# Modulation chunks 4 to 17 as multiply-adds on VectorE in place of matmuls on TensorE

## The chip, the cores and the metric

One core of a Trainium2 chip runs the whole kernel. The metric is the device time of one launch in microseconds (us). The engines are TensorE (PE; its weight loads are listed as PEld), VectorE (DVE), ScalarE (ACT), GpSimd (POOL) and SyncE (SP), whose queue issues the DMAs. Each engine works through its own queue in order, and semaphores make it wait for the others.

## The reference

One encoder layer works on 1024 prompt frames and 32 sample frames of width 1024, in float32. All three sub-layers are modulated by a condition vector `c`, one for the prompt and one for the sample:

```python
mod = jax.nn.silu(c) @ w_mod + b_mod          # (1, 1024) @ (1024, 9216)
sh1, sc1, g1, sh2, sc2, g2, sh3, sc3, g3 = jnp.split(mod, N_MOD, axis=-1)
h = adaln_in(x, gains[0], sh1, sc1)           # rmsnorm(x) * (1 + scale) + shift
x = x + FFN_RES * g1[:, None] * rmsnorm(swiglu(h, w1_gate, w1_up, w1_down), gains[1])
h = adaln_in(x, gains[2], sh2, sc2)           # then the two attention mixers, w_out, g2
h = adaln_in(x, gains[4], sh3, sc3)           # then the second feed-forward part, g3
```

The feed-forward width is 2816, that is 22 blocks of 128. `w_mod` has 37.7 MB of float32.

## The kernel before

Frames lie on the free axis, in three blocks of 384, 384 and 288 columns. Features lie on the 128 partitions. A float32 weight tile `raw` (128 partitions, 1024 elements each, 512 KB) is loaded from DRAM, and `split_w` (L253 to L259) splits it into a high part, written by ACT (L257), and a low part, written by DVE (L258). Each product is then three matmuls (`mm3`, L279 to L281).

**The feed-forward loop** (`ffn`, L479 to L560) takes the 22 blocks of the width in 11 groups of two (x and y). A group loads six weight tiles: gate and up of x and of y, and down of x and of y. For each block of frames it computes gate and up of x and y (`up`, 24 matmuls each for gate and up), then the down products (`down`, four pieces of 12 matmuls). `down` of one block runs behind the first `up` of the next one. In PSUM, gate and up rotate through three banks (`p1`). The down pieces rotate through two buffers (`p2`), and each is freed by a DVE addition into the accumulator `facc` (L535). DVE also multiplies `sl` by `up` (L505) and writes the low half of `gg` (L508), the operand of the down products.

**The modulation** has 18 chunks of 512 columns of `w_mod`. `mod_chunk` (L175 to L209) loads a chunk as two tiles of 1 MB from the pool of split weights (`wpool`, eight buffers) and multiplies it by `csil` on PE, 8 products in four groups of 32 output rows (L187). ACT copies the result (L190), PE transposes it in four pieces (L193), and DVE reduces it and adds the bias (L197, L199). For scales and gates DVE then writes `acoef` or `gcoef`. Chunks 0 to 3 run before the feed-forward part. Chunks 4 to 17 run two at a time, at the end of groups 2 to 8 of the first feed-forward part (`mod_rest`, L588 to L594).

**Side work** is cut into steps by generators. `step` (L431) takes one step of the first generator in the list. `up` calls two steps behind gate and two behind up (`PACE`), and `down` one behind each piece, so a group has 36 steps.

**Order.** SP's queue is written by hand until the end of the first group. Everything else is set by a scheduler that works through the program's order with modelled times. A tile of a pool waits until one of the pool's buffers is free: `rpool` has three buffers of 4 KB a partition, for the raw weights, and `hpool` has five.

Of the kernel before, what the change touches and what calls it, by code (L numbers as in the profile page):

```python
# [7 lines left out]
F32 = mybir.dt.float32  # L8
# [3 lines left out]
OP = mybir.AluOpType  # L12
AX = mybir.AxisListType
# [61 lines left out]
def encoder_step(ctx: ExitStack, tc, x_prompt, x_sample, cache_a_k, cache_a_v, cache_b_k, cache_b_v,  # L75
# [4 lines left out]
    te, ve, ae, ge, dma = nc.tensor, nc.vector, nc.scalar, nc.gpsimd, nc.sync  # L80
# [4 lines left out]
    rpool = ctx.enter_context(tc.tile_pool(name="rpool", bufs=3))  # L85
# [17 lines left out]
    def h_tile(shape, name, dt=F32):  # L103
        return hpool.tile(shape, dt, name=name, tag="h")
# [7 lines left out]
    def pc(name, shape=(128, 512)):  # L112
        return psc.tile(list(shape), F32, name=name, tag="pc")

    def p1(name, shape=(128, 512)):
        return ps1.tile(list(shape), F32, name=name, tag="p1")
# [27 lines left out]
    ident = consts.tile([128, 128], F32, name="ident")  # L144
# [18 lines left out]
    csil = consts.tile([128, KT, 32], F32, name="csil")  # L163
# [4 lines left out]
    modT = consts.tile([128, 2, 72], F32, name="modT")  # L168
# [3 lines left out]
    def gain(i):  # L172
        return cst[:, 72 + 8 * i:80 + 8 * i]

    def mod_chunk(n):  # L175
        raws = []
        for g in range(2):
            r = wpool.tile([128, 4, 512], F32, name="wm", tag="w")
            dma.dma_start(r, w_mod[0, 512 * g:512 * (g + 1), 512 * n:512 * (n + 1)]
                          .rearrange("(k p) n -> p k n", p=128))  # L180
            raws.append(r)
        bank = p1 if n < 4 else pc
        pm = bank("pm")
        for kk in range(2):
            for g in range(4):
                k = 2 * g + kk
                te.matmul(pm[32 * g:32 * g + 32, :], csil[:, k, :], raws[k // 4][:, k % 4, :],  # L187
                          start=kk == 0, stop=kk == 1)
        mr = h_tile([128, 512], "mr")
        ae.activation(mr, pm, AF.Copy)  # L190
        pt = bank("pmt", (128, 4, 128))
        for b in range(4):
            te.transpose(pt[:, b, :], mr[:, 128 * b:128 * b + 128], ident)  # L193
        seg, half = divmod(n, 2)
        c0 = 8 * seg + 4 * half
        cs, ks = slice(c0, c0 + 4), slice(4 * half, 4 * half + 4)
        ve.tensor_reduce(modT[:, :, cs], pt.rearrange("p b (g j) -> p j b g", g=4)[:, 0:2],  # L197
                         axis=AX.X, op=OP.add)
        ve.tensor_tensor(modT[:, :, cs], modT[:, :, cs],  # L199
                         cst[:, None, cs].to_broadcast([128, 2, 4]), op=OP.add)  # L200
        sub, kind = divmod(seg, 3)
        if kind == 1:
            ve.scalar_tensor_tensor(acoef[:, sub, :, ks], modT[:, :, cs], 1.0,
                                    gain(2 * sub)[:, None, ks].to_broadcast([128, 2, 4]),
                                    op0=OP.add, op1=OP.mult)
        elif kind == 2:
            ve.scalar_tensor_tensor(gcoef[:, sub, :, ks], modT[:, :, cs], 1.0 if sub == 1 else 0.5,
                                    gain(2 * sub + 1)[:, None, ks].to_broadcast([128, 2, 4]),
                                    op0=OP.mult, op1=OP.mult)  # L209


    ub = {}

    def bias_rows():
        ta = s_tile([8, 257], "ta")
        dma.dma_start(ta, rel_bias_a[0])
        ua = s_tile([8, 384], "ua")
        ve.memset(ua[:, 0:128], 0.0)
        ve.tensor_scalar(ua[:, 128:384], ta[:, 0:256], ta[:, 0:1], None, op0=OP.subtract)
        tt = s_tile([8, 32], "tt")  # L220
        dma.dma_start(tt, t5_bias_table)
        ubt = s_tile([8, 384], "ubt")
        for lo, hi, b in T5_RANGES:
            ve.tensor_copy(ubt[:, lo + 255:hi + 256], tt[:, b:b + 1].to_broadcast([8, hi - lo + 1]))
        ve.memset(ubt[:, 383:384], 0.0)
        for kind, u in (("A", ua), ("B", ubt)):
            ub[kind] = dram.tile([8, 128, 384], F32, name="skew_" + kind)
            dma.dma_start(ub[kind], u[:, None, :].to_broadcast([8, 128, 384]))
        sk = consts.tile([128, 8], F32, name="sk")
        dma.dma_start(sk, bass.AP(tensor=sinks_b.tensor, offset=sinks_b.offset, ap=[[0, 128], [1, 8]]))  # L230
        sks = consts.tile([64, 4], F32, name="sks")
        for h in range(2):
            dma.dma_start(sks[32 * h:32 * h + 32], bass.AP(tensor=sinks_b.tensor, offset=sinks_b.offset + h,
                                                          ap=[[0, 32], [2, 4]]))
        nsk = consts.tile([128, 8], F32, name="nsk")
        ve.tensor_scalar(nsk, sk, -1.0, None, op0=OP.mult)
        ub["sk"], ub["sks"], ub["nsk"] = sk, sks, nsk
# [210 lines left out]
    def begin(key, gen, first=False):  # L448
        side.insert(0 if first else len(side), marked(key, gen))

    def marked(key, gen):
        yield from gen
        done.add(key)
# [122 lines left out]
    def start(tb):  # L576
        if tb not in XIN:
            XIN[tb] = load_x(tb)
        yield from transpose_x(tb, *XIN[tb])
        yield from norm_h(XT[tb], tb, 0, H1, 0 if tb else 4)  # L580
        if tb == 2:
            for t in range(3):
                dma.dma_start(xs_dram[0][t], XT[t])
# [4 lines left out]
    def mod_rest(gi):  # L588
        if gi == 0:
            in_order.close()  # L590
            bias_rows()
        for n in (2 + 2 * gi, 3 + 2 * gi):
            if 4 <= n < 18:
                mod_chunk(n)  # L594

    ffn1 = ffn("h1", H1, F1, w1_gate, w1_up, w1_down, mod_rest, "h2", lambda tb: between(F1[tb], tb, 0, H2))
    first = start(0)
    for o in START:
        if o == "x":
            next(first)  # L600
        elif o == "n":
            for said in first:
                if said == "ahead":
                    break
        elif o == "w":
            next(ffn1)
        elif o == "y":
            XIN[1] = load_x(1)
        else:
            mod_chunk(int(o))  # L610
# [701 lines left out]
```

## Time and profile before

| | us |
|---|---|
| median of three runs | 2239.25 |
| lowest and highest run | 2239.08, 2243.16 |
| the profiled execution | 2243.16 |
| its span, first to last instruction | 2241.4 |
| PE busy in the span | 2179.2 |
| DVE busy in the span | 1086.7 |

The profile is that of the run with 2243.16 us. Its span leaves 1.76 us outside. In the stretch that the change touches, from 190 to 655 us, the page's slices show PE at 8 or 9 tenths and above, DVE at 3 tenths and POOL at 0.

### The profile page before, as it was taken

How to read it: one execution, taken by the hardware profiler on the slowest of the kernel's cores; microseconds unless marked ns; L12 is line 12 of the kernel's file. 1: busy time of each engine (PE TensorE's matmuls, PEld its weight loads, DVE VectorE, ACT ScalarE, POOL GpSimd, SP SyncE). 2: the span in 40 equal slices, each digit the busy share in tenths (PEclk: the TensorE clock that was granted, in tenths of full speed). 3: DMA queues.
4: the chain of work that ended last, by engine and by line, in shares of the span. 5: the costliest groups of instructions: out<-in, count | busy, mean ns of one | idle time of the engine just before them, and what ended most of it. 6: DMA issues, size and time to landing. Idle time of an engine off the chain costs nothing.

```text
span 2241.4 us, 34009 instructions
## 1 busy us (share of the span) xinstructions
PE 2179.2 (97%) x14180; PEld 2063.9 (92%) x14180; DVE 1086.7 (48%) x2187; ACT 703.7 (31%) x1464; POOL 179.0 (8%) x281
## 2 busy tenths in 40 slices
PE   6999999999999999899999899999999999999998
PEld 4998999999999999889788579999999999999998
DVE  5733333332344387677544775776433333333336
ACT  4411101210121254476544673533211111111133
POOL 1100000000000022100100322310000000000000
PEclk9999999999999999899999899999999999999999
DMA  9256223422232244100211211422311111111122
GB/s 317 95 76 187 75 95 95 132 76 94 94 115 74 71 141 158 59 27 23 67 30 30 77 55 59 158 83 88 101 57 38 38 44 51 57 38 50 45 65 82
DMA packets 199901, 186.00 MB, mean 83 GB/s; under 512 B 6892, under 2 KB 169092, under 8 KB 198596
## 3 DMA queue, kind: packets, MB, share of 16 engines
q1 hardware_dynamic: 199748, 183.84, 26.9%
q8 instruction: 111, 1.82, 0.3%
q14 instruction: 42, 0.34, 0.1%
HBM read 160.98 MB, written 22.84 MB: 82 GB/s over the span
## 4 chain that ended last, share of the span: by engine, by line
PE 89%; DVE 5%; DMA 3%; ACT 2%; issue 1%; POOL 0%; SPq 0%; DVEq 0%; ACTq 0%; POOLq 0%
PE up L279 7%; PE up L281 7%; PE gate L279 7%; PE gate L281 7%; PE up L280 7%; PE gate L280 7%; PE dn L279 7%; PE dn L280 7%; PE dn L281 7%; PE po L669 2%; PE S L708 2%; PE pq L279 2%; PE pq L280 2%; PE pq L281 2%; PE pm L187 1%; PE wo L279 1%
## 5 line engine op out<-in xcount | busy, mean ns | idle before, releaser
L535 DVE TENSOR_TENSOR facc<-dn,facc 128x768 f32<-128x768 f32 (+1 forms) x240 | 213.1, 889 | 285.9 <-PE dn L281 285.8
L280 PE MATMUL gate<-h_lo,w 128*128 128x384 f32 (+1 forms) x1056 | 340.5, 322 | 4.0 <-DVE h_lo L400 4.0
L279 PE MATMUL up<-h_hi,w 128*128 128x384 f32 (+1 forms) x1056 | 341.2, 323 | 0.0
L279 PE MATMUL dn<-gg,w 128*128 128x384 f32 (+1 forms) x1056 | 339.8, 323 | 0.9 <-DVE facc L535 0.8
L279 PE MATMUL gate<-h_hi,w 128*128 128x384 f32 (+1 forms) x1056 | 340.6, 323 | 0.0
L280 PE MATMUL dn<-gg,w 128*128 128x384 f32 (+1 forms) x1056 | 339.6, 322 | 0.6 <-DVE gg L508 0.6
L281 PE MATMUL gate<-h_hi,w 128*128 128x384 f32 (+1 forms) x1056 | 340.2, 322 | 0.0
L280 PE MATMUL up<-h_lo,w 128*128 128x384 f32 (+1 forms) x1056 | 339.8, 322 | 0.0
L281 PE MATMUL up<-h_hi,w 128*128 128x384 f32 (+1 forms) x1056 | 339.4, 321 | 0.0
L281 PE MATMUL dn<-gg,w 128*128 128x384 f32 (+1 forms) x1056 | 339.4, 321 | 0.0
L258 DVE TENSOR_TENSOR w<-raw,w 128x1024 fp32r<-128x1024 f32 x187 | 231.6, 1246 | 143.4 <-ACT w L257 143.2
L505 DVE TENSOR_TENSOR sl<-sl,up 128x384 f32<-128x384 f32 (+1 forms) x132 | 68.6, 520 | 421.5 <-PE up L281 421.1
L257 ACT ACTIVATE w<-raw 128x1024 fp32r<-128x1024 f32 x187 | 195.8, 1056 | 244.2 <-PE dn L281 94.9
L504 ACT ACTIVATE sl<-gate 128x384 f32<-128x384 f32 (+1 forms) x132 | 61.0, 462 | 612.8 <-PE gate L281 612.7
L279 PEld LDWEIGHTS gate<-h_hi,w 128*128 128x128 f32 x1056 | 198.4, 188 | 5.9 <-ACT gg L507 5.0
L279 PEld LDWEIGHTS up<-h_hi,w 128*128 128x128 f32 x1056 | 198.4, 188 | 5.9 <-issue 5.9
L280 PEld LDWEIGHTS gate<-h_lo,w 128*128 128x128 f32 x1056 | 198.3, 188 | 4.7 <-DVE h_lo L400 4.7
L279 PEld LDWEIGHTS dn<-gg,w 128*128 128x128 f32 x1056 | 198.7, 189 | 1.6 <-DVE facc L535 1.2
L280 PEld LDWEIGHTS dn<-gg,w 128*128 128x128 f32 x1056 | 198.7, 188 | 1.0 <-DVE gg L508 0.9
L281 PEld LDWEIGHTS up<-h_hi,w 128*128 128x128 f32 x1056 | 198.7, 188 | 0.0
L281 PEld LDWEIGHTS dn<-gg,w 128*128 128x128 f32 x1056 | 198.6, 188 | 0.0
L280 PEld LDWEIGHTS up<-h_lo,w 128*128 128x128 f32 x1056 | 198.5, 188 | 0.0
(219 smaller groups left out, 3212.6 us busy)
## 6 DMA issues: line engine op xcount, KB each, us to landing
wm<-in_w_mod_dram SPq DMA_DIRECT2D x36, 1024.0 KB, 7.2
raw<-in_w_gate_dram SPq DMA_DIRECT2D x54, 512.0 KB, 4.7
raw<-in_w_up_dram SPq DMA_DIRECT2D x54, 512.0 KB, 35.1
raw<-in_w_down_dram SPq DMA_DIRECT2D x54, 512.0 KB, 4.6
raw<-in_w_in_dram SPq DMA_DIRECT2D x18, 512.0 KB, 3.9
raw<-in_w_out_dram SPq DMA_DIRECT2D x13, 512.0 KB, 3.6
xr<-xs SPq DMA_DIRECT2D x16, 384.0 KB, 5.0
raw<-xs SPq DMA_DIRECT2D x8, 512.0 KB, 4.5
```

The lines of the kernel that those rows point to most:

```text
L187: te.matmul(pm[32 * g:32 * g + 32, :], csil[:, k, :], raws[k // 4][:, k % 4, :], start=kk == 0, stop=kk == 1)
L257: ae.activation(w[:, 0], r, AF.Copy)
L258: ve.tensor_sub(w[:, 1], r, w[:, 0])
L279: te.matmul(ps, w[:, 0, k], hi, start=start, stop=False)
L280: te.matmul(ps, w[:, 0, k], lo, start=False, stop=False)
L281: te.matmul(ps, w[:, 1, k], hi, start=False, stop=stop)
L504: ae.activation(sl[:, :w], ps[0][:, :w], AF.Silu)
L505: ve.tensor_tensor(sl[:, :w], sl[:, :w], ps[1][:, :w], op=OP.mult)
L535: ve.tensor_tensor(o, ps[:, :, :w], o, op=OP.add)
L669: te.matmul(po[64 * h:64 * h + 64, :n], vsl(j, h, kn), PT(h, j, kn), start=j == 0, stop=j == nt - 1)
L708: te.matmul(S[:, c:ce], self.T[:, h, :], KQ[:, 0, 128 * k0 + c:128 * k0 + ce], start=True, stop=True)
```

## The change

Chunks 0 to 3 stay as they are, all in `p1` banks. Chunks 4 to 17 go through a new generator, `mod_aside`. It loads a chunk as four tiles of 512 KB from `rpool`. DVE multiplies each slab of 128 rows by the column of `csil` that belongs to it and adds the product to an accumulator, one accumulator (`macc`, from `hpool`) for the prompt and one for the sample. That makes 16 operations of 128x512 for a chunk. PE then transposes each accumulator in four pieces into the single `pc` bank, and DVE reduces each over the 128 values that were partitions. The rest (`coefs`) is as before. The generator is begun once, at the end of the second group, and takes 15 steps for a chunk.

```diff
+    def mod_aside(n):
+
+        acc = [h_tile([128, 512], "macc") for _ in range(2)]
+        for g in range(4):
+            r = rpool.tile([128, 2, 512], F32, name="raw", tag="r")
+            dma.dma_start(r, w_mod[0, 256 * g:256 * (g + 1), 512 * n:512 * (n + 1)]
+                          .rearrange("(k p) n -> p k n", p=128))
+            for kk in range(2):
+                k = 2 * g + kk
+                for j in range(2):
+                    c = csil[:, k, j:j + 1]
+                    if k == 0:
+                        ve.tensor_scalar(acc[j], r[:, kk], c, None, op0=OP.mult)
+                    else:
+                        ve.scalar_tensor_tensor(acc[j], r[:, kk], c, acc[j], op0=OP.mult, op1=OP.add)
+            yield
+            yield
+            yield
+        yield
+        yield
+        c0 = 4 * n
+        for j in range(2):
+            pt = pc("pmt", (128, 4, 128))
+            for b in range(4):
+                te.transpose(pt[:, b, :], acc[j][:, 128 * b:128 * b + 128], ident)
+            ve.tensor_reduce(modT[:, j, c0:c0 + 4], pt, axis=AX.X, op=OP.add)
+        coefs(n)
+        yield
+
+    def mod_all(first, last):
+        for n in range(first, last):
+            yield from mod_aside(n)
...
         if gi == 0:
             in_order.close()
             bias_rows()
-        for n in (2 + 2 * gi, 3 + 2 * gi):
-            if 4 <= n < 18:
-                mod_chunk(n)
+        if gi == 1:
+            begin("mod", mod_all(4, 18))
```

The scheduler moves the rest. Three places show how. In the rows of the changed kernel the line numbers are its own: L220 to L240 are in `mod_aside`, L292 to L295 in `split_w`, L316 to L318 in `mm3`, L542 and L545 in `up` and L572 in `down`.

On SP's queue, in the middle of the first feed-forward part, before:

```order
L255 DMA raw<-in_w_gate_dram 128x8x128
L179 DMA wm<-in_w_mod_dram 128x4x512 x4
L255 DMA raw<-in_w_up_dram 128x8x128
L255 DMA raw<-in_w_down_dram 128x1024 x2
L255 DMA raw<-in_w_gate_dram 128x8x128
L255 DMA raw<-in_w_up_dram 128x8x128
L255 DMA raw<-in_w_gate_dram 128x8x128
```

and now:

```order
L292 DMA raw<-in_w_down_dram 128x1024 x2
L220 DMA raw<-in_w_mod_dram 128x2x512 x10
L292 DMA raw<-in_w_gate_dram 128x8x128
L292 DMA raw<-in_w_up_dram 128x8x128
L292 DMA raw<-in_w_gate_dram 128x8x128
L292 DMA raw<-in_w_up_dram 128x8x128
L292 DMA raw<-in_w_down_dram 128x1024 x2
```

Eight to ten loads of the modulation now stand in one row between the six weights of a group and those of the next, in six groups (10, 10, 9, 10, 9 and 8), and all of them use the three `raw` buffers.

On DVE, behind the last `up` (128x288) of a group, before:

```order
L258 TENSOR_TENSOR w<-raw,w 128x1024
L508 TENSOR_TENSOR gg<-sl,gg 128x288
L258 TENSOR_TENSOR w<-raw,w 128x1024 x2
L197 TENSOR_REDUCE modT<-pmt 128x2x4
L199 TENSOR_TENSOR modT<-modT,cst 128x2x4
L505 TENSOR_TENSOR sl<-sl,up 128x384
L258 TENSOR_TENSOR w<-raw,w 128x1024
L535 TENSOR_TENSOR facc<-dn,facc 128x576
L258 TENSOR_TENSOR w<-raw,w 128x1024
L535 TENSOR_TENSOR facc<-dn,facc 128x576
L508 TENSOR_TENSOR gg<-sl,gg 128x384
```

and now, in the second of the six groups:

```order
L295 TENSOR_TENSOR w<-raw,w 128x1024
L545 TENSOR_TENSOR gg<-sl,gg 128x288
L227 TENSOR_SCALAR macc<-raw,csil 128x512 x2
L229 SCALAR_TENSOR_TENSOR macc<-raw,csil,macc 128x512 x8
L542 TENSOR_TENSOR sl<-sl,up 128x384
L229 SCALAR_TENSOR_TENSOR macc<-raw,csil,macc 128x512 x2
L572 TENSOR_TENSOR facc<-dn,facc 128x576
L545 TENSOR_TENSOR gg<-sl,gg 128x384
L229 SCALAR_TENSOR_TENSOR macc<-raw,csil,macc 128x512
L227 TENSOR_SCALAR macc<-raw,csil 128x512
L229 SCALAR_TENSOR_TENSOR macc<-raw,csil,macc 128x512
L572 TENSOR_TENSOR facc<-dn,facc 128x576
```

Multiply-adds now stand ahead of the additions that free the down buffers, about 40 of them in the first half of such a group.

On PE, at the last `up` (128x288) of a group, before:

```order
L281 MATMUL up<-h_hi,w 128x288
L187 MATMUL pm<-wm,csil 32x512 x8
L279 MATMUL gate<-h_hi,w 128x384
L280 MATMUL gate<-h_lo,w 128x384
L279 MATMUL dn<-gg,w 128x288
```

and now, where a transposition of the same group stands between two down pieces:

```order
L318 MATMUL dn<-gg,w 128x288
L318 MATMUL gate<-h_hi,w 128x384
L239 MATMUL pmt<-ident,macc 128x128 x4
L316 MATMUL dn<-gg,w 128x288
L317 MATMUL dn<-gg,w 128x288
```

The 8 products of a chunk are gone from PE's queue, and two transpositions of four pieces stand there for each chunk where one stood.

## Rows read from the trace of the kernel before

**Rows 1.** The page: busy us, share and instructions of each engine.

```profile
PE 2179.2 (97%) x14180; PEld 2063.9 (92%) x14180; DVE 1086.7 (48%) x2187; ACT 703.7 (31%) x1464; POOL 179.0 (8%) x281
```

**Rows 2.** Windows: PE, PEld, DVE, ACT, POOL busy, PE clock, DMA share, GB/s.

```profile
200.00:300.00 100.00, 100.00 (x639) 94.92 (x638) 32.76 (x51) 17.09 (x27) 0.00 (x0) 1.00 0.35 111
```

**Rows 3.** Timeline, ACT's silu behind each group's last gate (start, duration; first and second part).

```profile
184.63 0.41 ACT L504 ACTIVATE sl<-gate 128x288 f32<-128x288 f32 x1 [10.52 <-PE gate L281]
...
261.86 0.41 ACT L504 ACTIVATE sl<-gate 128x288 f32<-128x288 f32 x1 [10.58 <-PE gate L281]
...
335.97 0.41 ACT L504 ACTIVATE sl<-gate 128x288 f32<-128x288 f32 x1 [10.58 <-PE gate L281]
...
1651.90 0.41 ACT L504 ACTIVATE sl<-gate 128x288 f32<-128x288 f32 x1 [10.18 <-PE gate L281]
...
1720.92 0.41 ACT L504 ACTIVATE sl<-gate 128x288 f32<-128x288 f32 x1 [10.18 <-PE gate L281]
```

**Rows 4.** Timeline of PE, a chunk's products and transpositions among the matmuls (start, duration).

```profile
264.66 0.29 PE L281 MATMUL up<-h_hi,w 128*128 128x288 f32 x1
264.88 1.92 PE L187 MATMUL pm<-wm,csil 128*32 128x512 f32 x16
266.74 0.44 PE L279 MATMUL gate<-h_hi,w 128*128 128x384 f32 x1
267.02 0.33 PE L280 MATMUL gate<-h_lo,w 128*128 128x384 f32 x1
...
271.82 0.60 PE L193 MATMUL pmt<-ident,mr 128*128 128x128 f32 x4
...
272.43 0.34 PE L280 MATMUL up<-h_lo,w 128*128 128x384 f32 x1
```

**Rows 5.** Timeline of PE at the first of the 14 chunks.

```profile
187.49 0.29 PE L281 MATMUL up<-h_hi,w 128*128 128x288 f32 x1
...
190.81 1.91 PE L187 MATMUL pm<-wm,csil 128*32 128x512 f32 x12 [1.67 <-DMA wm<-in_w_mod_dram]
...
192.65 0.44 PE L279 MATMUL gate<-h_hi,w 128*128 128x384 f32 x1
```

**Rows 6.** Groups of DVE by shape: count, busy us, mean ns of one, idle before.

```profile
L258 DVE TENSOR_TENSOR w<-raw,w 128x1024 fp32r<-128x1024 f32 x187 | 231.6, 1246 | 143.4 <-ACT w L257 143.2
L535 DVE TENSOR_TENSOR facc<-dn,facc 128x576 f32<-128x576 f32 x80 | 60.1, 754 | 69.1 <-PE dn L281 69.1
L508 DVE TENSOR_TENSOR gg<-sl,gg 128x384 fp32r<-128x384 f32 x88 | 48.9, 556 | 39.7 <-ACT gg L507 39.7
L773 DVE TENSOR_REDUCE nmb<-Sb 128x2 f32<-128x512 f32 x28 | 19.2, 686 | 0.6
L1106 DVE SCALAR_TENSOR_TENSOR z<-o,cst,rstd 128x384 f32<-128x384 f32 x16 | 13.1, 863 | 0.0
L1271 DVE SCALAR_TENSOR_TENSOR xp<-py,ry,xp 128x512 f32<-128x512 f32 x16 | 11.5, 743 | 0.0
```

**Rows 7.** Timeline of DVE: multiply-adds pairs back to back, with the row behind each.

```profile
1263.12 1.18 DVE L1106 SCALAR_TENSOR_TENSOR z<-o,cst,rstd 128x384 f32<-128x384 f32 x2
1264.22 0.41 DVE L659 COPY PT<-pp 128x256 f32<-128x256 f32 x1
...
2217.63 0.16 DVE L290 TENSOR_TENSOR rt<-ry 128x3 f32<-128x3 f32 x1
2217.82 0.16 DVE L291 SCALAR_TENSOR_TENSOR rt<-rt,rv 128x3 f32<-128x3 f32 x1
...
2230.91 1.40 DVE L1271 SCALAR_TENSOR_TENSOR xp<-py,ry,xp 128x512 f32<-128x512 f32 x2
2232.23 0.15 DVE L342 TENSOR_SCALAR rv<-pss 128x2 f32<-128x2 f32 x1
```

**Rows 8.** DMA issues: KB each, median us from issue to landing.

```profile
wm<-in_w_mod_dram SPq DMA_DIRECT2D x36, 1024.0 KB, 7.2
raw<-in_w_gate_dram SPq DMA_DIRECT2D x54, 512.0 KB, 4.7
```

More of the change, by code (lines that the diff above doesn't have):

```diff
@@ L181, in mod_chunk @@
             raws.append(r)
-        bank = p1 if n < 4 else pc
-        pm = bank("pm")
+        pm = p1("pm")
         for kk in range(2):
@@ L190, in mod_chunk, with coefs @@
         ae.activation(mr, pm, AF.Copy)
-        pt = bank("pmt", (128, 4, 128))
+        pt = p1("pmt", (128, 4, 128))
         for b in range(4):
             te.transpose(pt[:, b, :], mr[:, 128 * b:128 * b + 128], ident)
+        cs = slice(4 * n, 4 * n + 4)
+        ve.tensor_reduce(modT[:, :, cs], pt.rearrange("p b (g j) -> p j b g", g=4)[:, 0:2],
+                         axis=AX.X, op=OP.add)
+        coefs(n)
+    def coefs(n):
         seg, half = divmod(n, 2)
@@ L196, in mod_chunk @@
         cs, ks = slice(c0, c0 + 4), slice(4 * half, 4 * half + 4)
-        ve.tensor_reduce(modT[:, :, cs], pt.rearrange("p b (g j) -> p j b g", g=4)[:, 0:2],
-                         axis=AX.X, op=OP.add)
         ve.tensor_tensor(modT[:, :, cs], modT[:, :, cs],
@@ L209, in mod_chunk @@
                                     op0=OP.mult, op1=OP.mult)
+    def mod_aside(n):
[23 more added lines that the diff above has]
+            ve.tensor_reduce(modT[:, j, c0:c0 + 4], pt, axis=AX.X, op=OP.add)
+        coefs(n)
+        yield
+    def mod_all(first, last):
+        for n in range(first, last):
+            yield from mod_aside(n)
     ub = {}
```

## The prediction, made before the changed kernel ran

> **What bounds the kernel now.** I read the page's busy times first. PE works in 97% of the span [rows 1]. A window in the part that the change touches shows it full, at a granted clock of 1.00, with DVE busy for a third, ACT for a sixth and POOL for nothing [rows 2]. So in this part PE's own instructions are the time. What the modulation costs there is read from the period of a group. ACT's silu behind the last gate of a group marks it. In the first part, with two chunks in each group, the period is 335.97 - 261.86 = 74.11 us. In the second part, which has the same matmuls and no modulation, it is 1720.92 - 1651.90 = 69.02 us [rows 3]. The two chunks cost 5.09 us, or 2.55 us each. That is a price on the path, since the matmuls of the two periods are the same otherwise.
>
> The timeline splits this price. A group has 144 matmuls for each block of frames (six weights, 8 slabs, 3 matmuls), so 288 of 384 columns and 144 of 288. Over 69.02 us that is 0.454 ns a column, 0.174 us for a matmul of 384 and 0.131 us for one of 288. The products of a chunk stretch the way from the last `up` to the second `gate` behind them to 267.02 - 264.66 = 2.36 us, where 0.131 + 0.174 would stand, so they cost 2.06 us. A transposition in four pieces stretches the way to the second matmul behind it to 272.43 - 271.82 = 0.61 us, where 0.174 would stand, so it costs 0.44 us [rows 4]. Together that is 2.50 us, against 2.55 from the periods.
>
> **The change part by part: PE.** Fourteen chunks leave the stream: 14 x 2.55 = 35.7 us. Each comes back as two transpositions of 0.44 us: 14 x 0.88 = 12.3 us. The net gain is 23.4 us. The first of the 14 chunks costs more now: from the last `up` to the `gate` behind the products it takes 192.65 - 187.49 = 5.16 us, of which 0.13 are the `up`'s own. So it took 5.03 us in place of 2.06, because its loads landed late [rows 5]. The other 3.0 us go too, since no matmul reads those loads any more. The periods agree: 77.23 us from 184.63 to 261.86, which is 3.1 over the next one [rows 3]. Gain on PE: 26.4 us. ACT loses 14 copies, which nothing in these windows waits for, at a sixth busy.
>
> **DVE.** A chunk brings 16 operations of 128x512 and two reductions of 128x512. The nearest row for a multiply-add of this size is the one of the last stage, 0.743 us, with one operand in PSUM; a reduction takes 0.686 us [rows 6]. Back to back they cost less: two multiply-adds of 512 columns take 1.40 us, and the operation behind them starts 1.32 us after the first; two of 384 columns that read only SBUF take 1.10 us up to the next, 0.55 each, which is 0.68 with 128 more columns at 1 ns each [rows 7]. I take 0.67 us. The accumulators alternate, so each multiply-add needs the result of the one before last, and its wait should be over when its turn comes. A chunk is then 16 x 0.67 + 2 x 0.6 + 0.3 = 12.2 us of DVE, and all are 171 us over some 430 us in which DVE is busy for a third: about 73%. There is room on average.
>
> But it isn't spread evenly. All loads of the modulation in a group stand ahead of the next group's weights in the three `raw` buffers, and DVE's order puts some 40 multiply-adds into the first half of a group. I walked the second of the six groups by the new order and the rows' durations. From the end of the last `up` of 288 columns PE issues 48 matmuls of gate and up, 24 of down and 23 of gate: 8.3 + 3.1 + 4.0 = 15.4 us. Then its third down piece wants the buffer that the first `facc` addition frees. In front of that DVE has `sl` and `gg` of 288 columns (0.4 each), a low half of weights (1.14), twelve operations of `macc` (8.0), an `sl` (0.47) and the addition itself (0.67): 11.1 us back to back, at 0.09 us less than the single durations [rows 6, 7]. The slack is 4.3 us. Two loads that wait for each other eat it. At the start of the group two of the three `raw` buffers hold the down weights, so the next load of the modulation can start only when the last one has been used up. A load of this size lands 4.7 us after its issue [rows 8]; with 0.4 us for the issue I take 5.1. DVE's other work covers 3 us of each, so it waits about 2 us twice. The first wait pushes a block of four multiply-adds and a low half of weights past the end of the last `up`, so that DVE begins the stretch 2.7 us late; the second falls into the stretch. The first addition then comes 0.3 us late and the second some 0.6. In the first of the six groups the same walk gives 1.1 us, where two weight loads of the next group follow each other through one buffer and their low halves stand ahead of `facc`. In the fourth it gives 0. I charge 0.8 us a group and 0.2 for a transposition that finds its bank or accumulator late: 6 x 0.9 = 5.4 us.
>
> **The rest.** The loads of the next group's weights come later than now, but their first matmul stands some 20 us behind the end of their split in these walks: nothing. The four 1 MB buffers a group that leave the pool of split weights free it: nothing, since the raw buffers hold the weights back. Behind the first part the same instructions stand in an order that differs in 65 places on PE's queue. I can't sign that; I keep 4 us to either side, the distance of the highest run from the other two.
>
> **Sum.** Against the profiled execution: 2243.16 - 26.4 + 5.4 = 2222.2 us. It lies 3.9 us over the median, and no row says where; the changed kernel's time will be a median too, so I take the gain from that: 2239.25 - 21.0 = 2218.2 us. **Forecast: 2218 us**, by itself 2209 to 2231.
>
> **The rivals.** First, **DVE's multiply-adds don't overlap**, and the gain is lost in front of the down pieces. Dependent operations show the price: 0.16 us long, they start 0.19 us apart [rows 7], so a full-length one would take 0.743 + 0.035 = 0.78 us. That is 0.11 more for each of some 40 in a burst, 4.4 us a group, and 6 x 4.4 = 26 us: 2244 us. All new multiply-adds carry a wait on DVE itself, which speaks for it; the alternation of the accumulators speaks against it. A mean of 0.863 us stands for multiply-adds of 384 columns from SBUF [rows 6], but those run while POOL works beside them; POOL is at 0 here [rows 2].
>
> The Trainium skill, "VectorE: DVE Perf Modes", section "The DRAIN you can't avoid", says that after each operation the pipeline is emptied before the next one starts, and that chaining without semaphores does not avoid it. By that rule a pace below the duration would not exist, this rival would hold, and the time would be its 2244 us. The pairs of the trace, 1.32 us for two of 0.743, speak against it. The same section of the Trainium skill also grants an earlier start to an operation that isn't held.
>
> Second, **the loads are late, and the kernel is slower.** The three `raw` buffers are the place: two serial loads a group stand ahead of DVE's additions, so every us by which a load lands later costs 2 us a group, 12 us in all. The 1 MB loads of the same matrix land after 7.2 us [rows 8]. With 0.4 for the issue that is 2.5 us more than I take, or 30 us: 2248 us. It decides from a landing 1.8 us later than mine, 6.9 us. Against it: the new loads have half the bytes, and the weights of that size land in 4.7.
>
> Third, **the change doesn't do what it says**: PE's freed time isn't given back, because a wait that the products now cover comes up in their place at the group's end. Then 2239. The second part's period of 69.02 us, with the same products and no modulation, speaks against it.
>
> Fourth, DVE is never late: 2239.25 - 26.4 = 2213 us. It lies within the forecast's own range.
>
> **How the numbers follow.** I give the forecast with the fourth case 0.70, the first rival 0.13, the second 0.12, the third 0.05. For 8 in 10 the range goes from 2209 (all of the gain and 4 us of luck behind the first part) to 2244, the first rival's time; most of the second and a little below 2209 are left out. About what a measurement of this kernel can tell is 0.2%, 4.5 us. Faster than 2234.8: nearly all of the forecast and a little of the first two rivals, 0.71. Slower than 2243.7: half of the first and most of the second, 0.16. Within: 0.13.
>
> **What would show it.** Right: group periods of 69.02 + 2.33 x 0.88 = 71.1 us and up to 1 us more in the six groups, multiply-adds of 0.74 us that start 0.67 us apart, DVE at about 7 tenths in that stretch, and PE's waits for `facc` at some 5 us in all. Wrong by the first rival: starts 0.78 us apart and PE waiting for `facc` 4 us and more in each group. Wrong by the second: DVE idle for DMA in front of `macc`, with landings of 7 us. If PE's idle time in the first part stays small and the total still isn't near 2218, the later stages have moved, and my 4 us for them were too few.

## The result and the profile after

The changed kernel takes **2230.64 us** (median of 5 runs, 2222.83 to 2232.07), the kernel before 2239.25 (5 runs beside them, 2237.14 to 2244.28). The ratio is 0.9947 [0.9923, 0.9971]. That is faster by 8.6 us, where 21 were forecast. The profiled execution took 2232.07 us, its span is 2230.3.

ACT's silu (`sl`) marks the same places in both programs, so the span can be cut into stretches. The first mark is the first 288-column silu at the end of the first group, the second the silu of [rows 3] at 184.63, the third a 384-column silu in the tenth group. From the timeline of ACT, of before:

```profile
107.71 0.41 ACT L504 ACTIVATE sl<-gate 128x288 f32<-128x288 f32 x1 [6.11 <-PE gate L281]
...
709.42 0.49 ACT L504 ACTIVATE sl<-gate 128x384 f32<-128x384 f32 x1 [0.26 <-PE gate L281]
```

and of after:

```profile
109.00 0.41 ACT L541 ACTIVATE sl<-gate 128x288 f32<-128x288 f32 x1 [6.11 <-PE gate L318]
...
197.64 0.41 ACT L541 ACTIVATE sl<-gate 128x288 f32<-128x288 f32 x1 [7.45 <-PE gate L318]
...
271.35 0.41 ACT L541 ACTIVATE sl<-gate 128x288 f32<-128x288 f32 x1 [11.07 <-PE gate L318]
...
342.42 0.41 ACT L541 ACTIVATE sl<-gate 128x288 f32<-128x288 f32 x1 [10.18 <-PE gate L318]
...
699.34 0.49 ACT L541 ACTIVATE sl<-gate 128x384 f32<-128x384 f32 x1 [0.30 <-PE gate L318]
```

| stretch | before, us | after, us | difference | forecast |
|---|---|---|---|---|
| start to the first mark | 107.71 | 109.00 | +1.29 | 0 |
| to the second mark (second group) | 76.92 | 88.64 | **+11.72** | 0 |
| to the third mark (the chunks' groups) | 524.79 | 501.70 | **-23.09** | -21.0 |
| to the end of the span | 1531.98 | 1530.96 | -1.02 | 0 |
| sum | 2241.40 | 2230.30 | -11.10 | -21.0 |

So the part that the prediction worked out came, 2 us better than forecast. Half of it was lost again in the group before, in which the change computes nothing. The differences at both ends are no more than the executions differ anyway: in the seven traces of changed kernels below, the first mark lies between 106.67 and 108.71 us and the last stretch takes 1527 to 1534 us. The windows of that group and of the stretch behind it show the same (PE, PEld, DVE, ACT, POOL busy, PE clock, DMA share, GB/s), first of before:

```profile
100.00:185.00 85.00, 85.00 (x542) 85.00 (x541) 30.87 (x75) 11.23 (x21) 0.68 (x2) 1.00 0.46 75
185.00:640.00 455.00, 453.03 (x2886) 430.29 (x2886) 152.18 (x218) 80.83 (x127) 0.00 (x0) 1.00 0.33 106
```

then of after:

```profile
100.00:185.00 85.00, 75.83 (x468) 75.51 (x468) 29.64 (x74) 13.17 (x23) 1.29 (x2) 0.94 0.43 64
185.00:640.00 455.00, 452.73 (x2866) 451.09 (x2865) 310.33 (x469) 76.08 (x117) 0.00 (x0) 1.00 0.38 114
```

What PE waited for in after, from 60 to 930 us (us in total, times, longest):

```profile
PE up L316 <- ACT sl L541: 9.2, 1, 9.2
PE dn L316 <- DVE facc L572: 3.5, 4, 1.6
```

One wait of 9.2 us for a silu is new. The timeline of ACT in after shows why the silu was late:

```profile
137.11 1.06 ACT L294 ACTIVATE w<-raw 128x1024 fp32r<-128x1024 f32 x1 [7.51 <-PE dn L318]
154.86 1.06 ACT L294 ACTIVATE w<-raw 128x1024 fp32r<-128x1024 f32 x1 [16.69 <-DMA raw<-in_w_up_dram]
155.82 0.47 ACT L541 ACTIVATE sl<-gate 128x384 f32<-128x384 f32 x1
```

ACT stands for 16.69 us in front of the conversion of an `up` weight of the next group, whose load hasn't landed. The silu behind it in ACT's queue runs at 155.82. In before the same silu runs at 137.65, as soon as its gate is done, and the first conversion comes only at 184.94:

```profile
137.65 0.49 ACT L504 ACTIVATE sl<-gate 128x384 f32<-128x384 f32 x1 [9.35 <-PE gate L281]
...
184.94 1.05 ACT L257 ACTIVATE w<-raw 128x1024 fp32r<-128x1024 f32 x1
```

Gate and up rotate through three banks, so PE goes on through `up` and the next gate and then has no free bank, which is the wait of 9.2 us. The order of ACT's instructions in the two timelines tells the same, from 122 us on (`w` is a conversion):

```
before: sl  gg  sl  gg  sl  gg  sl  gg  sl  gg  sl  w  w
after:  sl  gg  w   w   sl  gg  sl  gg ...
```

In before, the four 1 MB `wm` tiles of chunks 4 and 5 hold four of the eight buffers of the pool of split weights up to the end of the second group, so the next group's weights find no buffer until then. In after, those buffers are free (the first of the two conversions, at 137.11, starts when a down product is done, which frees its buffer), and the scheduler, which works with modelled times, puts two conversions ahead of a silu. That the buffers are the reason is tested below. The load is late because of what stands around it in SP's queue: the two writes of the rows of the biases (`skew_A` and `skew_B`, 1.5 MB each, `bias_rows`). The timeline of SP in after, and the load's piece of the chain of waits (start, duration):

```profile
118.44 0.82 SPq L265 DMA_DIRECT2D skew_A<-ua  x1
119.57 4.82 SPq L292 DMA_DIRECT2D raw<-in_w_up_dram  x1
124.44 21.45 SPq L265 DMA_DIRECT2D skew_B<-ubt  x1
```

```profile
119.57 35.20 DMA raw<-in_w_up_dram
```

A load of this size that lands in 4.7 us elsewhere [rows 8] takes 35.20 beside those writes. In before it takes as long (a median of 35.1 us for the `up` loads from 100 to 190 us), but nobody there wants it early.

PE pays a little more than the wait. Windows of after around it (same columns):

```profile
150.00:155.00 5.00, 0.00 (x0) 0.00 (x0) 0.00 (x0) 0.14 (x1) 0.00 (x0) 0.59 0.50 100
...
157.00:159.00 2.00, 2.00 (x8) 2.00 (x7) 1.20 (x3) 0.90 (x2) 0.00 (x0) 0.50 0.47 50
159.00:161.00 2.00, 2.00 (x8) 2.00 (x8) 0.00 (x0) 0.00 (x0) 0.00 (x0) 0.50 0.47 50
161.00:163.00 2.00, 2.00 (x13) 2.00 (x13) 0.00 (x0) 0.00 (x0) 0.00 (x0) 0.98 0.52 65
```

While PE idles, the granted clock falls from 1.00 to 0.50, that is from 2.4 to 1.2 GHz, and comes back at 161 us, 4.7 us after PE's restart at 156.35. The fourteen matmuls in between, 0.32 us apart and more, take 4.6 us in place of 14 x 0.174 = 2.4, which costs 2.2 us. With the 9.2 us that is 11.4 of the 11.7 us.

DVE's new work in after, from 185 to 640 us (count, busy us, mean ns of one, idle before):

```profile
L229 DVE SCALAR_TENSOR_TENSOR macc<-raw,csil,macc 128x512 f32<-128x512 f32 x196 | 137.8, 747 | 19.0 <-DMA raw<-in_w_mod_dram 18.7
...
L240 DVE TENSOR_REDUCE modT<-pmt 128x4 f32<-128x512 f32 x28 | 19.2, 684 | 4.1 <-PE pmt L239 4.1
...
L227 DVE TENSOR_SCALAR macc<-raw,csil 128x512 f32<-128x512 f32 x28 | 12.8, 482 | 7.3 <-DMA raw<-in_w_mod_dram 7.2
```

and four multiply-adds back to back, with the row behind them, which starts 2.66 us after the first, so 0.665 us for each:

```profile
265.12 2.74 DVE L229 SCALAR_TENSOR_TENSOR macc<-raw,csil,macc 128x512 f32<-128x512 f32 x4 [0.52 <-DMA raw<-in_w_mod_dram]
267.78 0.95 DVE L572 TENSOR_TENSOR facc<-dn,facc 128x768 f32<-128x768 f32 x1
```

### The profile page after: what moved, and what is told of

Same layout as the page of the kernel before. It is cut to its first block, busy times and chain, and to the rows that moved or that the text cites. A ratio compares the mean times of both kernels' runs of the same rounds, so it can differ in the third digit from the quotient of the medians.

```text
span 2230.3 us, 33962 instructions
## 1 busy us (share of the span) xinstructions
PE 2163.1 (97%) x14012; PEld 2069.8 (93%) x14012; DVE 1238.6 (56%) x2425; ACT 698.1 (31%) x1450; POOL 180.5 (8%) x281
## 4 chain that ended last, share of the span: by engine, by line
PE 84%; DMA 7%; DVE 6%; ACT 1%; issue 1%; POOL 1%; SPq 0%; DVEq 0%; ACTq 0%; POOLq 0%
PE dn L316 7%; PE up L316 7%; PE up L318 7%; PE up L317 7%; PE dn L317 7%; PE dn L318 7%; PE gate L318 7%; PE gate L317 7%; PE gate L316 7%; DMA raw<-in_w_up_dram 4%; PE po L705 3%; PE S L744 2%; PE pq L316 2%; PE pq L318 2%; PE pq L317 2%; PE pp L768 1%
## 5 line engine op out<-in xcount | busy, mean ns | idle before, releaser
L316 PE MATMUL up<-h_hi,w 128*128 128x384 f32 (+1 forms) x1056 | 341.1, 323 | 9.2 <-ACT sl L541 9.2
L316 PE MATMUL dn<-gg,w 128*128 128x384 f32 (+1 forms) x1056 | 340.8, 324 | 3.9 <-DVE facc L572 3.5
L316 PE MATMUL gate<-h_hi,w 128*128 128x384 f32 (+1 forms) x1056 | 341.2, 323 | 0.0
L318 PE MATMUL up<-h_hi,w 128*128 128x384 f32 (+1 forms) x1056 | 340.4, 322 | 0.0
L318 PE MATMUL gate<-h_hi,w 128*128 128x384 f32 (+1 forms) x1056 | 340.4, 322 | 0.0
L318 PE MATMUL dn<-gg,w 128*128 128x384 f32 (+1 forms) x1056 | 339.4, 321 | 0.0
L572 DVE TENSOR_TENSOR facc<-dn,facc 128x768 f32<-128x768 f32 (+1 forms) x240 | 212.7, 888 | 221.4 <-PE dn L318 221.3
L295 DVE TENSOR_TENSOR w<-raw,w 128x1024 fp32r<-128x1024 f32 x187 | 232.3, 1250 | 170.7 <-ACT w L294 163.6
L542 DVE TENSOR_TENSOR sl<-sl,up 128x384 f32<-128x384 f32 (+1 forms) x132 | 68.5, 519 | 282.3 <-PE up L318 282.0
L316 PEld LDWEIGHTS up<-h_hi,w 128*128 128x128 f32 x1056 | 199.1, 189 | 9.5 <-ACT sl L541 9.5
L316 PEld LDWEIGHTS dn<-gg,w 128*128 128x128 f32 x1056 | 198.7, 189 | 5.8 <-DVE facc L572 4.8
L317 PEld LDWEIGHTS dn<-gg,w 128*128 128x128 f32 x1056 | 198.7, 188 | 1.2 <-DVE gg L545 1.2
L318 PEld LDWEIGHTS up<-h_hi,w 128*128 128x128 f32 x1056 | 199.4, 189 | 0.0
L316 PEld LDWEIGHTS gate<-h_hi,w 128*128 128x128 f32 x1056 | 198.9, 188 | 0.1
L318 PEld LDWEIGHTS gate<-h_hi,w 128*128 128x128 f32 x1056 | 198.7, 188 | 0.0
```

The source lines that it names most:

```text
L295: ve.tensor_sub(w[:, 1], r, w[:, 0])
L316: te.matmul(ps, w[:, 0, k], hi, start=start, stop=False)
L317: te.matmul(ps, w[:, 0, k], lo, start=False, stop=False)
L318: te.matmul(ps, w[:, 1, k], hi, start=False, stop=stop)
L542: ve.tensor_tensor(sl[:, :w], sl[:, :w], ps[1][:, :w], op=OP.mult)
L572: ve.tensor_tensor(o, ps[:, :, :w], o, op=OP.add)
```

## The experiments

Two things had to be told apart: whether the 11.7 us come from the conversions that moved ahead of a silu, and from which of their two conditions (free buffers, late load); and whether DVE's new work costs more than it seems.

### The bias rows later

```diff
         if gi == 0:
             in_order.close()
+        if gi == 7:
             bias_rows()
```

> The changed kernel with the bias rows (and their two 1.5 MB writes to DRAM) moved from the end of the first group to the end of the eighth; ACT's order at the second group stays that of the changed kernel, with the high halves of the next gate and up weights ahead of a silu. Theory (in the changed kernel ACT stands in front of that silu until 154.86 us for an up tile that was issued at 119.57 behind the first bias write, and PE stands 9.2 us behind it): that wait of PE is gone, the silu that started at 155.82 starts near 140, and the time falls by 10 to 12 us to about 2219. Rival (the wait belongs to the conversions' place alone, whatever the load does): the 9.2 us stay and the time stays at 2230. A second way to miss: the writes now hold up a load behind the eighth group, and a wait of PE appears after 640 us.

Measured: 2248.27 us, ratio 1.0036 [1.0022, 1.0051]. It missed the 2219, by the second way that the expectation names. In the second group all came as expected, and the window is full again:

```profile
100.00:185.00 85.00, 85.00 (x541) 85.00 (x540) 35.18 (x50) 15.15 (x25) 1.29 (x2) 1.00 0.19 56
```

ACT has the two conversions ahead of the silu as in after, but here the `up` load, issued at 119.23, lands after 3.8 us, and the silu runs at 138.72:

```profile
136.81 2.01 ACT L294 ACTIVATE w<-raw 128x1024 fp32r<-128x1024 f32 x2 [7.51 <-PE dn L318]
138.72 0.47 ACT L541 ACTIVATE sl<-gate 128x384 f32<-128x384 f32 x1
```

So the order alone costs nothing; it takes the late load as well. But the writes now stand among the loads of the ninth group, where conversions stand ahead of silus too. PE's waits from 185 to 930 us, and ACT there:

```profile
PE dn L316 <- DVE facc L572: 22.2, 3, 21.2
PE up L316 <- ACT sl L541: 6.7, 1, 6.7
```

```profile
647.74 1.06 ACT L294 ACTIVATE w<-raw 128x1024 fp32r<-128x1024 f32 x1 [14.25 <-DMA raw<-in_w_up_dram]
...
679.19 1.06 ACT L294 ACTIVATE w<-raw 128x1024 fp32r<-128x1024 f32 x1 [27.73 <-DMA raw<-in_w_gate_dram]
```

The longer wait has the same root on another engine: DVE's low half of the late weight stands ahead of the additions that free the down buffers. From the timeline of DVE:

```profile
680.28 1.22 DVE L295 TENSOR_TENSOR w<-raw,w 128x1024 fp32r<-128x1024 f32 x1 [28.61 <-ACT w L294]
...
683.60 1.81 DVE L572 TENSOR_TENSOR facc<-dn,facc 128x768 f32<-128x768 f32 x2
```

The silus that served as marks lie at 108.70, 185.67 and 716.99 us here. The second group takes 76.97 us, 11.67 less than in after. The stretch to the third mark takes 531.32, 29.6 more: the waits of 21.2 and 6.7 us, some 2 us of the lower clock behind each, less 2.3 us of waits for `facc` that after has there and this kernel hasn't. So the early loss goes when the writes go, and the same writes cost more at the later place, where two late loads hold PE up.

### Two chunks back on PE

```diff
         if gi == 1:
-            begin("mod", mod_all(4, 18))
+            mod_chunk(4)
+            mod_chunk(5)
+            begin("mod", mod_all(6, 18))
```

(with `pm` and `pmt` of these two in the `pc` bank, as before)

> The changed kernel with chunks 4 and 5 left on PE at the end of the second group, as before the change, and 6 to 17 on VectorE. Their four 1 MB tiles take buffers of the pool of split weights again, and ACT's order at the second group is that of the kernel before, with the two conversions behind four more silus. Theory (freed buffers let the scheduler move the conversions forward, in front of a load that lands late): no wait of PE for ACT near 146 us; gain against before 12 x 1.67 = 20 us less 2 for the down pieces, so about 2221, in spite of two chunks more on PE than the changed kernel. Rival (the new loads or DVE work cost the missing 12 us): 2230 + 2 x 1.67 + 3.0 = about 2236.

Measured: 2221.16 us, ratio 0.9914 [0.9896, 0.9932], as expected. The writes and the late load are still there; only the four `wm` tiles hold their buffers again. The wait for ACT is gone, and the only thing that PE waits for from 100 to 640 us is the load of chunks 4 and 5:

```profile
100.00:185.00 85.00, 85.00 (x541) 85.00 (x540) 31.32 (x77) 11.38 (x21) 1.29 (x2) 1.00 0.45 71
```

```profile
PE pm L187 <- DMA wm<-in_w_mod_dram: 2.0, 2, 1.7
```

This kernel beats both. But it differs from the changed one in two ways at once, in the buffers and in the two chunks.

### No chunks 4 to 17 at all

```diff
         if gi == 1:
-            begin("mod", mod_all(4, 18))
+            ve.memset(modT[:, :, 16:72], 0.0)
+        for n in (2 + 2 * gi, 3 + 2 * gi):
+            if 4 <= n < 18:
+                coefs(n)
```

> Chunks 4 to 17 of the modulation are left out altogether (their rows of modT are zero; bias and coefficients stay), so there are no loads, no products, no multiply-adds and no transpositions of them. ACT's order at the second group is that of the changed kernel. Theory (freed buffers): the wait of some 9 us near 146 us is there without any of the new work, and the time is 2239.25 - 35.7 - 3.0 + 11.7 = about 2212. Rival (the wait comes from the new loads or the DVE work): no such wait, and 2239.25 - 38.7 = about 2200.5.

Measured: 2212.88 us, ratio 0.9881 [0.9861, 0.9901]. Without a single new load, multiply-add or transposition the wait is still there:

```profile
PE up L316 <- ACT sl L541: 8.2, 1, 8.2
```

```profile
100.00:185.00 85.00, 76.84 (x475) 76.52 (x474) 28.53 (x72) 13.36 (x21) 0.67 (x2) 0.94 0.46 73
```

So the loss doesn't need what the change adds. It comes from what it takes away. (This kernel leaves work out, so its time says nothing about the change's worth.)

### Fewer multiply-adds

```diff
-                for j in range(2):
+                for j in range(2 if k == 0 else 1):
```

> The changed kernel with half of the multiply-adds: the sample's accumulator gets only its first slab, so 7 of 16 operations of a chunk are left out; loads, transpositions and reductions stay. Theory (DVE's lateness costs 2.3 us in the six groups, the rest of the miss is the one wait at 146 us): 0 to 3 us under the changed kernel, and the 9.2 us wait stays. Rival (the multiply-adds on DVE cost most of the missing 12 us): 8 to 12 us under it, 2219 to 2222.

Measured: 2233.23 us, ratio 0.9966 [0.9955, 0.9977], so no gain on the changed kernel's 2230.64: 2.6 us above it, where 0 to 3 under it were expected. DVE has a fifth less to do, and PE waits as long (the window, then the waits from 60 to 930 us):

```profile
185.00:640.00 455.00, 451.24 (x2848) 449.50 (x2847) 251.28 (x371) 74.41 (x117) 0.00 (x0) 1.00 0.37 112
```

```profile
PE up L316 <- ACT sl L541: 9.7, 1, 9.7
PE dn L316 <- DVE facc L572: 4.4, 3, 3.2
```

DVE's throughput is not what holds the kernel. The waits for `facc` don't shrink either (4.4 us against 3.5). From 185 to 640 us they go with the stall ahead of them and not with the number of multiply-adds: 3.2 us here behind 9.7, 2.3 in after behind 9.2, 0.5 behind 5.4 in the kernel of the next section, and none in the two kernels that have all multiply-adds and no stall (the bias rows later, the buffers held).

### The writes from ACT's queue

```diff
-            dma.dma_start(ub[kind], u[:, None, :].to_broadcast([8, 128, 384]))
+            ae.dma_start(ub[kind], u[:, None, :].to_broadcast([8, 128, 384]))
```

> The changed kernel with one edit: the two writes of bias rows at the end of the first group are issued from ACT's queue in place of SP's. ACT's order still has the two conversions of the next group's weights ahead of a silu. Theory (the up load stands behind the first write in the queue that they share, and landed 35.20 us after its issue for that): the load lands in some 5 us, ACT doesn't wait for it, the stretch from 100 to 185 us has PE full at 1.00, and the time falls by the 9.2 us of the wait and the 2 us of the lower clock that follows it: 2219 to 2221 us. Rival (the write takes the bandwidth of the DMA engines, whichever queue it was issued from): the load still lands after 30 us and more, the wait of 8 to 10 us for ACT stays, and the time is 2229 to 2232.

Measured: 2225.73 us (2219.78 to 2228.69), ratio 0.9934 [0.9921, 0.9947], between the two. The wait is smaller, not gone:

```profile
PE up L316 <- ACT sl L541: 5.4, 1, 5.4
```

```profile
150.43 1.06 ACT L294 ACTIVATE w<-raw 128x1024 fp32r<-128x1024 f32 x1 [12.93 <-DMA raw<-in_w_up_dram]
```

```profile
118.86 0.40 SPq L292 DMA_DIRECT2D raw<-in_w_up_dram  x1
```

The load, issued at 118.86, now stands in another queue than the writes, and it still lands 150.4 - 118.9 = 31.5 us after its issue, against 35.2. So another queue is worth 3.7 us, and the load is late beside the writes whichever queue they stand in. The windows differ (same columns, after and then this kernel):

```profile
140.00:144.00 4.00, 4.00 (x25) 4.00 (x24) 0.00 (x0) 0.00 (x0) 0.00 (x0) 1.00 0.46 49
140.00:144.00 4.00, 4.00 (x25) 4.00 (x24) 0.00 (x0) 0.00 (x0) 0.00 (x0) 1.00 0.51 66
```

In these 4 us one queue for both moves 49 GB/s. With the writes in a queue of their own 66 move, and the 17 more are loads that run beside the writes. The Trainium skill, "DMA: Bandwidth & Descriptors", section "Issuing engines are not separate DMA queues", says that transfers started by different engines run on the same 16 DMA engines and interleave there; the 31.5 us agree. The rival was right on the landing, and wrong on the wait and on the time by 4 us, since it left out what the common queue adds: the wait is 3.8 us shorter, and so is the second group (84.80 us against 88.64). The edit has a side effect, 7.2 us in which ACT issues the second write; the silu behind it is some 5 us late, and PE doesn't wait for that one.

The same edit in the kernel with two chunks on PE:

> Chunks 4 and 5 on PE, 6 to 17 on VectorE (the kernel of 2221.16 us), with the two writes of bias rows issued from ACT's queue. In that kernel ACT's order has the silus ahead of the late conversions, so that nothing waits for the writes. Theory: the queue is worth only what PE waited for behind the writes, the 2.0 us for the tile of the first chunk, so 2219 to 2221. Rival (the late loads cost more than the waits of PE show): 2214 or less.

Measured: 2221.15 us, ratio 0.9912 [0.9899, 0.9925], the same as the 2221.16 without it. In the trace PE's 2.0 us for the tiles of chunks 4 and 5 are gone (PE is full from 185 to 640 us), but two us are less than the two intervals can tell. Where ACT's order doesn't put the conversion ahead of the silu, the queue of the writes is worth no more than that; the rival's 2214 fell.

### The buffers held, all 14 chunks on DVE

This undoes the freed buffers where the stall is and leaves all new work in place: at the end of the second group four tiles are taken from the pool, each with a load of 16 KB and a matmul of 8 columns. In the groups behind it the buffers stay free.

```diff
         if gi == 1:
+            pm = pc("pm")
+            for k in range(4):
+                r = wpool.tile([128, 4, 512], F32, name="wm", tag="w")
+                dma.dma_start(r[:, :, 0:8], w_mod[0, 0:512, 8 * k:8 * k + 8]
+                              .rearrange("(k p) n -> p k n", p=128))
+                te.matmul(pm[0:32, 8 * k:8 * k + 8], csil[:, k, :], r[:, 0, 0:8],
+                          start=True, stop=True)
             begin("mod", mod_all(4, 18))
```

> The changed kernel, with all 14 chunks on VectorE, and one addition: at the end of the second group four tiles of the pool of split weights are taken as the kernel before took them, each with a load of 16 KB and one matmul of 8 columns, whose results nobody reads. The order of ACT up to the end of the second group is then that of the kernel before: the two conversions stand behind the silus of the group. Theory (the freed buffers let the conversions move ahead of a silu, and that cost 11.7 us): PE is full from 100 to 185 us at 1.00, no wait for ACT, and the time is 2230.64 - 11.7 = 2219 us, 2217 to 2221 with the four small loads and matmuls. Rival (the loss there has another cause, or comes back later): the 100 to 185 us have a wait of 8 us and more again, or the time is 2227 to 2232.

Measured: **2215.54 us** (2210.91 to 2216.99) against 2241.83 for the kernel before on the same chip, ratio 0.9875 [0.9857, 0.9893]: faster by 26.3 us, the best of the kernels that compute everything, and 1.5 us below the 2217 to 2221 expected. ACT runs the silu that was late as soon as its gate is done, and both windows are full:

```profile
138.43 0.49 ACT L541 ACTIVATE sl<-gate 128x384 f32<-128x384 f32 x1 [9.34 <-PE gate L318]
```

```profile
100.00:185.00 85.00, 85.00 (x541) 85.00 (x541) 31.33 (x76) 11.16 (x21) 1.29 (x2) 1.00 0.44 64
185.00:640.00 455.00, 455.00 (x2892) 454.10 (x2892) 314.79 (x475) 80.69 (x122) 0.00 (x0) 1.00 0.39 116
```

Its marks stand at

```profile
108.49 0.41 ACT L541 ACTIVATE sl<-gate 128x288 f32<-128x288 f32 x1 [6.12 <-PE gate L318]
...
185.41 0.41 ACT L541 ACTIVATE sl<-gate 128x288 f32<-128x288 f32 x1 [10.52 <-PE gate L318]
...
256.88 0.41 ACT L541 ACTIVATE sl<-gate 128x288 f32<-128x288 f32 x1 [11.07 <-PE gate L318]
...
684.59 0.49 ACT L541 ACTIVATE sl<-gate 128x384 f32<-128x384 f32 x1 [0.30 <-PE gate L318]
```

From the first to the second mark it takes 76.92 us, the same as before to the hundredth: the 11.72 are gone. From the second to the third it takes 499.18, 25.6 less than before and 2.5 less than after. Behind that it takes 2215.2 - 684.59 = 1530.6 us, where before takes 1532.0 and after 1531.0. The 15.1 us between its span and that of after are 11.72 + 2.52 + 0.51 ahead of the first mark + 0.35 behind the third; 11.7 were expected. The 2.52 are mostly the waits for `facc` behind the stall.

## Why the prediction was right and wrong

**The time inside the range: luck.** 2230.64 us lies at the upper edge of the prediction's 2209 to 2231, with 8.6 us of gain where 21 were forecast. What ate the rest is a stall in a place where the prediction had put the cost at nothing.

**PE's gain: right.** 26.4 us were counted for the 14 chunks, and the kernel with held buffers gives 25.6 from its second mark (185.41 us) to the tenth group, without one wait of PE from 100 to 640 us. The group periods of after (271.35 to 342.42 is 71.07 us, the following ones 70.8 to 71.7) lie close to the 71.1 and up to 1 us more that were expected, two of them 0.3 under.

**DVE's pace: right.** The multiply-adds are 0.747 us long and start 0.665 us apart, where 0.74 and 0.67 were written; DVE is busy for 68% of the stretch. The first rival (0.78 us apart, 2244 us) fell with that. The Trainium skill, "VectorE: DVE Perf Modes", section "The DRAIN you can't avoid", says that the next operation starts only when the pipeline has emptied, and that one that is not held starts earlier; the four rows back to back, 0.665 us apart at 0.747, show the earlier start and not the rule.

**The charge for late additions: too high.** 5.4 us were taken. (That is 6 x 0.9; the parts that it names, 0.8 and 0.2 a group, make 6.0, and the forecast 2219.) PE waits 2.3 us for `facc` from 185 to 640 us in after, 3.5 with the groups behind, and not at all in that stretch with held buffers. The size that was off is the load: 4.0 us from issue to landing in the median (3.6 to 6.6), where 5.1 stood for issue and landing. At the prediction's own price of 2 us a group for each us, the difference covers its 0.8 a group; that is an estimate, and no run slowed the loads down. The 2.3 us of after are one more consequence of the stall: they fall into the first of the six groups, which takes 271.35 - 197.64 = 73.71 us there and 256.88 - 185.41 = 71.47 with held buffers, and the kernel with the later writes, which has all the new work and no stall there, has none of them. The second rival (landings from 6.9 us on, 2248 us) fell too; the fourth, DVE never late, is what the kernel with held buffers shows.

**The step that failed** is in "The rest": "The four 1 MB buffers a group that leave the pool of split weights free it: nothing, since the raw buffers hold the weights back." The `raw` buffers do hold the loads back, but two of the next group's weights had theirs already. What held those two was the pool of split weights. Freed, the scheduler put their conversions ahead of a silu on ACT, and one of the loads is the one that shares the DMA engines with 3 MB of writes. In place of the prediction's nothing it cost 11.72 us and the 2.3 behind it. Four runs show it from different sides: without the added work the wait stays (8.2 us), without the writes there it goes, with the two chunks back it goes, and with nothing but the buffers held it goes.

The order of ACT's queue in the changed program and the trace of before, with its landing of 35 us, would have shown it beforehand. The prediction looked at the orders of SP, DVE and PE in the six groups where the chunks are computed, and took ACT, a sixth busy, as an engine that nothing waits for. It looked for the cost where instructions were added, and not at the first place where buffers come free.

**The sum.** By the marks the profiled executions differ by 11.1 us: 23.1 gained, 11.7 lost, 1.3 lost ahead of the first mark and 1.0 gained behind the third; the last two are within what single executions differ by. The 4 us kept for the later stages were enough. The prediction's last sign, a miss with PE's idle time in the first part still small, did not come: PE idled there, 9.2 us in one wait. The medians differ by 8.6, since the profiled execution of before lies 3.9 us above its median and that of after 1.4. The five runs of after spread over 9 us, at mean granted clocks from 0.982 to 0.988, the shortest at the highest; whether the stall is shorter in the short runs is not shown, since only one execution has a trace. The third rival, that freed time isn't given back, came out by half, but in another place and by another mechanism than the one that it named.

## What to carry to other kernels

When a change frees buffers, look for the first instruction that they let through, on every engine and ahead of the changed place too: an engine that is a sixth busy still stalls everything behind it if its next instruction waits for a late load. Where a static scheduler works with modelled times, a transfer that lands far later than the model thinks (here 35 us beside large writes) is safe only while something else holds its consumer back. To find such a thing, cut both spans at the same landmarks and compare stretch by stretch; the loss showed at once in a stretch in which nothing had been changed.

## What the runs showed of the hardware

While the two writes of 1.5 MB to DRAM run, the DMA engines move no more than 49 to 50 GB/s in most slices, at a busy share of 0.46 to 0.47 (the windows of after from 157 to 161 us), so more than half of the engines' time stays unused. A 512 KB load issued among them takes 35.2 us all the same, or 31.5 from another queue than theirs, where 3.8 stand without the writes. From two queues 66 GB/s move in the window above. Which of the 16 engines the writes use, and how these divide their time, wasn't tried.

A wait of PE of 9.2 us brought the granted clock down to 0.50, and PE's matmuls behind it ran at half speed for a while; two waits in the kernel with the later writes (6.7 and 21.2 us) did the same. Each cost some 2 us on top of its wait.
